# A tile of sparse attention moved among the query projections, and its output sums moved to GpSimd

## The chip, the cores and the metric

The kernel runs on one core of one Trainium2 chip. Times are device microseconds (us) of one execution of the whole program. TensorE (PE in the profile) multiplies matrices into PSUM, VectorE (DVE), ScalarE (ACT) and GpSimd (POOL) work on tiles, SyncE (SP) issues nearly all loads from HBM. Each engine works through its own queue in order, and waits where an instruction needs something that another engine or a load has not yet delivered.

## The reference

Two decoder layers over 512 tokens of width 1024. Layer 0 has latent attention, layer 1 sparse attention; each is followed by cross-attention into 256 memory tokens and a SwiGLU, with a residual and a layer norm after every sub-layer. All is float32. The change is in layer 1's sparse attention, 16 query heads in 4 groups that share keys and values:

```
def dsa_mixer(x, pos, rel_bias, w_in, w_o):
    h = x @ w_in          # -> q (16 heads x 64), k, v (4 x 64), q_idx (8 x 64), k_idx (64), w_idx (8)
    def one_block(...):   # 128 queries
        dots = einsum('bqhd,bkd->bqhk', qi_blk, k_idx) * 64 ** -0.5
        score = einsum('bqh,bqhk->bqk', wi_blk, relu(dots)); score = where(causal, score, -inf)
        _, sel = top_k(score, 128)                       # the keys of a query
        logits = einsum('bqngd,bqknd->bqngk', qg, k_sel) * 64 ** -0.5
        bias = rel_bias[t5_bucket(pos_blk - pos_sel)]
        p = softmax(where(sel_ok, logits + bias, -inf))
        return einsum('bqngk,bqknd->bqngd', p, v_sel)
    return blocks @ w_o
```

## The kernel before

A float32 product is made of reduced-precision ones: each operand is split into a high part (a rounding copy on ScalarE, `split`, line 98) and a low part (a subtraction on VectorE or GpSimd, line 100), and `mm3` (lines 121 to 123) adds three matmuls in PSUM. `chunk` loads 128x1024 weights into one of three raw buffers and splits them. The recording layer keeps each engine's queue roughly in the order of the source, but may put an instruction that it holds ready ahead of one that it holds late; within a queue nothing moves after that.

The sparse attention layer goes through these stages:

- Values, indexer keys and indexer queries are projected, and `masks[1]` to `masks[3]` collect the index scores of query tiles 1 to 3 (128 queries each; tile 0 needs only the causal mask).
- `topk` finds the 128 best keys of each query by 16 steps per tile. A step is a max of 8 and a replacement (lines 964, 965), both on VectorE; after the sixteenth, line 969 makes the mask. These 48 steps stand in `todo` and are handed out: 2 before each of the two key projections, `NTK` = 5 before each of the eight query projections, the last 4 in the item loop.
- Eight query projections (loop at line 1002), two heads each: 24 matmuls, then `stack_q_pool` with three copies on ScalarE and two subtractions on GpSimd. The weights' low parts are made on GpSimd too.
- 16 items, one for each query tile `qt` and key group `g`. `dsa_scores` (`run_s`) adds mask, and Q times both parts of K, for four heads, on PSUM banks of tag `b`; VectorE adds the bias and takes the maximum (line 410), ScalarE the exponential (416). Item i of tile 0 needs the heads 4i to 4i+3, so two query projections. `dsa_t` (`run_t`) spreads the reciprocal sums on GpSimd (421), transposes the probabilities on TensorE into banks of tag `a` and splits them. `dsa_pv` multiplies with the values: the high halves' sums are in partitions 0 to 63 of the bank `po`, the low halves' in 64 to 127.
- `out_proj` multiplies the outputs `OTd` with the output weights.

There are four PSUM banks of each tag, and 39 buffers of `t2` and 9 of `t8`; a tile waits until a buffer's last reader is done.

Of the kernel before, what the change touches and what calls it, by code (L numbers as in the profile page):

```python
# [12 lines left out]
FR = mybir.dt.float32r  # L13
I32 = mybir.dt.int32
AF = mybir.ActivationFunctionType
ALU = mybir.AluOpType
# [4 lines left out]
P = 128  # L21
# [3 lines left out]
NK = D // P  # L25
# [41 lines left out]
def tile_hybrid_mla_dsa_deepnorm_block(ctx: ExitStack, tc: tile.TileContext, A: dict, out: bass.AP):  # L67
    nc = tc.nc
# [13 lines left out]
    def t2(dt=F32, shape=(P, 512)):  # L82
        return tp.tile(list(shape), dt, tag="t2", name=nm("t2"), bufs=39)

    def t8(dt=FR, shape=(P, 4, 512)):
        return tp.tile(list(shape), dt, tag="t8", name=nm("t8"), bufs=9)
# [4 lines left out]
    def bank(tag, shape=(P, 512)):  # L91
        return pp.tile(list(shape), F32, tag=tag, name=nm("ps"))
# [14 lines left out]
    def chunk(src, shape, eng=None, after=(None, None)):  # L107
        n = int(np.prod(shape[1:]))
        raw = wp.tile([P, 1024], F32, tag="raw", name=nm("raw"), bufs=3)
        with behind(after[0]):  # L110
            nc.sync.dma_start(raw[:, :n], src)
        h = wp.tile([P, 1024], FR, tag="wh", name=nm("wh"))
        l = wp.tile([P, 1024], FR, tag="wl", name=nm("wl"))
        split(h[:, :n], l[:, :n], raw[:, :n], eng, after[1])
        if len(shape) == 2:
            return h[:, :n], l[:, :n]
        k = shape[1]
        return (h[:, :n].rearrange("p (k m) -> p k m", k=k), l[:, :n].rearrange("p (k m) -> p k m", k=k))
# [272 lines left out]
    def proj_tiles(ws, XT, halves):  # L391
        pss = [bank("a") for _ in ws]
        if halves:
            for cols in HALVES:
                for ps, w in zip(pss, ws):
                    proj(ps, w, XT, cols)
        else:
            for ps, w in zip(pss, ws):
                proj(ps, w, XT, (0, 512))
        return pss  # L400
# [34 lines left out]
    XT = [(t8(), t8()) for _ in range(2)]  # L435
# [41 lines left out]
    for c in range(4):  # L477
# [12 lines left out]
        for i in range(2):  # L490
            k = 2 * c + i
# [14 lines left out]
    steps = trig()  # L506
# [17 lines left out]
    OF = {}  # L524
# [141 lines left out]
    for h in range(16):  # L666
        PT = mla_t(h, Ss.pop(h))
# [45 lines left out]
    def cross(i, XT, m, kv0):  # L713
# [3 lines left out]
        def q_proj(hd):  # L717
            ws = [chunk(A["xa_q"][i, 2 * hd + dt], (P, NK, P)) for dt in range(2)]
            pq = proj_tiles(ws, XT, hd == 0)
            Q = []  # L720
            for dt in range(2):
                q = (t2(FR), t2(FR))
                split(q[0], q[1], pq[dt])
                Q.append(q)
            return Q

        def scores(hd, Q):
            Kt = kvs[hd][0]
# [164 lines left out]
    XT = norm.XT  # L893
# [8 lines left out]
    def stack_q_pool(ps, QA, QB):  # L902
        f = t2()
        nc.scalar.copy(f, ps)
        nc.scalar.copy(QA[0:64], ps[0:64])
        nc.scalar.copy(QB[64:128], ps[64:128])
        nc.gpsimd.tensor_tensor(QA[64:128], f[0:64], QA[0:64].bitcast(F32), op=ALU.subtract)
        nc.gpsimd.tensor_tensor(QB[0:64], f[64:128], QB[64:128].bitcast(F32), op=ALU.subtract)
# [50 lines left out]
    def topk(qt, its):  # L959
        n = P * (qt + 1)  # L960
        acc = masks[qt]
        for it in its:
            m8 = tp.tile([P, 8], F32, tag="m8", name=nm("m8"), bufs=4)
            nc.vector.max(out=m8, in_=acc[:, :n])  # L964
            nc.vector.match_replace(out=acc[:, :n], in_to_replace=m8, in_values=acc[:, :n], imm_value=-3e38)  # L965
        if its[-1] < TOPK // 8 - 1:
            return
        mk = MK[:, qt]
        nc.vector.tensor_scalar(mk[:, :n], acc[:, :n], -2e38, -BIG, op0=ALU.is_gt, op1=ALU.mult)
        masks[qt] = mk  # L970

    todo = [(qt, [i]) for qt in range(1, NT) for i in range(TOPK // 8)]
    NTK, NTI = 5, 1
# [16 lines left out]
    def dsa_bias(qt, g):  # L990
        n = P * (qt + 1)
        c0 = 127 + 384 - 128 * qt
        bt = t8(F32, (P, 4, 512)) if qt else t2(F32, (P, 4, P))
        read = nc.sync.dma_start(bt[:, :, 0:n],
                                 scr[bass.ds(r * (1 + qt), 1), 4 * g:4 * g + 4, :, c0:c0 + n].rearrange("a h p k -> p (a h) k"))
        reads.append(read)
        return bt

    Q = []
    q8 = t8()  # L1000
    first_bias, reads, spreads = [], [], []
    for j in range(8):
        if j >= 4:
            first_bias.append(dsa_bias(0, j - 4))
        for _ in range(min(NTK, len(todo))):
            topk(*todo.pop(0))
        (pq,) = proj_tiles([chunk(A["w_q"][j], (P, NK, P), nc.gpsimd)], XT, False)
        if j < 2:
            qa, qb = q8[:, 2 * j], q8[:, 2 * j + 1]
        else:  # L1010
            qa, qb = t2(FR), t2(FR)
        stack_q_pool(pq, qa, qb)
        Q += [qa, qb]

    OTd = []

    def new_outputs():
        o8 = t8()
        OTd.extend([(o8[:, 0], o8[:, 1]), (o8[:, 2], o8[:, 3])] + [(t2(FR), t2(FR)) for _ in range(NK - 2)])


    def dsa_scores(qt, g):
        n = P * (qt + 1)
# [28 lines left out]

    def dsa_pv(qt, g, rb, PT):
        ts_ = slice(P * qt, P * qt + P)
        po = bank("a")
        for kb in range(qt + 1):
            nc.tensor.matmul(po, VD[:, kb, g], PT[kb][0], start=(kb == 0), stop=False)
            nc.tensor.matmul(po, VD[:, kb, g], PT[kb][1], start=False, stop=(kb == qt))
        tmp = t2()
        nc.scalar.copy(tmp[0:64], po[64:128])  # L1060
        OF = t2(F32, (P, 2, P))
        ov = po[0:64].rearrange("p (i j q) -> p i j q", j=2, q=P)
        tv = tmp[0:64].rearrange("p (i j q) -> p i j q", j=2, q=P)
        for e in range(2):
            nc.vector.tensor_tensor(OF[64 * e:64 * e + 64], ov[:, :, e], tv[:, :, e], op=ALU.add)
        pr_ = bank("a", (P, 2, P))
        for i in range(2):
            nc.tensor.transpose(pr_[:, i], rb[:, 2 * i:2 * i + 2].rearrange("p a b -> p (a b)"), ident)
        nc.vector.tensor_tensor(OF, OF, pr_, op=ALU.mult)
        for i in range(2):  # L1070
            oh_, ol_ = OTd[2 * g + i]
            if qt < 3:
                nc.gpsimd.tensor_copy(oh_[:, ts_], OF[:, i])
                nc.gpsimd.tensor_tensor(ol_[:, ts_], OF[:, i], oh_[:, ts_].bitcast(F32), op=ALU.subtract)
            else:
                split(oh_[:, ts_], ol_[:, ts_], OF[:, i])


    items = [(qt, g) for qt in range(NT) for g in range(4)]
    LA = 12  # L1080
    Ss, PT = {}, {}

    def run_s(i):
        if i < 16:
            Ss[i] = dsa_scores(*items[i])

    def run_t(i):
        PT[i] = dsa_t(*items[i], Ss.pop(i))

    run_s(0)  # L1090
    run_s(1)
    run_t(0)
    new_outputs()
    for i in range(16):
        a = 1 if i < LA else 0
        if i != LA:
            run_s(i + 1 + a)
            run_t(i + a)
        dsa_pv(*items[i], *PT.pop(i))
        for _ in range(NTI):  # L1100
            if todo:
                topk(*todo.pop(0))
# [94 lines left out]
```

## Time and profile before

| what | value |
|---|---|
| median of 3 runs | 1549.07 us (1548.76 to 1550.13) |
| profiled execution, its time | 1550.88 us |
| its span (first to last instruction) | 1549.1 us |
| TensorE busy | 1510.6 us, 98% |
| VectorE, ScalarE, GpSimd busy | 64%, 42%, 21% |
| chain that ended last: TensorE, VectorE | 80%, 10% |

The profile comes from one execution, whose time lies 1.8 us above the median; terms read from it are differences within it. A matmul counts as busy until its modelled end, so that two which follow each other overlap: the pace of matmuls is read from their starts. The chain that ended last is followed back from the last instruction, at each step to what released it.

### The profile page before, as it was taken

How to read it: one execution, taken by the hardware profiler on the slowest of the kernel's cores; microseconds unless marked ns; L12 is line 12 of the kernel's file. 1: busy time of each engine (PE TensorE's matmuls, PEld its weight loads, DVE VectorE, ACT ScalarE, POOL GpSimd, SP SyncE). 2: the span in 40 equal slices, each digit the busy share in tenths (PEclk: the TensorE clock that was granted, in tenths of full speed). 3: DMA queues.
4: the chain of work that ended last, by engine and by line, in shares of the span. 5: the costliest groups of instructions: out<-in, count | busy, mean ns of one | idle time of the engine just before them, and what ended most of it. 6: DMA issues, size and time to landing. Idle time of an engine off the chain costs nothing.

```text
span 1549.1 us, 20803 instructions
## 1 busy us (share of the span) xinstructions
PE 1510.6 (98%) x7940; PEld 1290.5 (83%) x7940; DVE 996.6 (64%) x1709; ACT 650.1 (42%) x1150; POOL 321.8 (21%) x332
## 2 busy tenths in 40 slices
PE   9999999999999999999999899999999999999997
PEld 8788888988888888888888688898988888888886
DVE  6888868554746565654668979675548465656535
ACT  4677743343233333332246478334332333333320
POOL 2322101000132331400124553010002322324003
PEclk9999999999999999999999999999999999999999
DMA  6234424322323232223242337333323232322321
GB/s 221 71 99 110 147 82 139 120 87 91 130 88 116 75 121 86 98 90 109 83 150 69 96 109 245 109 109 110 109 90 128 78 113 94 106 94 88 96 94 55
DMA packets 51321, 166.79 MB, mean 108 GB/s; under 512 B 5300, under 2 KB 11748, under 8 KB 49172
## 3 DMA queue, kind: packets, MB, share of 16 engines
q1 hardware_dynamic: 50788, 164.41, 31.7%
q8 instruction: 62, 1.02, 0.3%
q10 hardware_dynamic: 432, 1.05, 0.2%
q14 instruction: 39, 0.32, 0.1%
HBM read 161.20 MB, written 9.47 MB: 110 GB/s over the span
## 4 chain that ended last, share of the span: by engine, by line
PE 80%; DVE 10%; ACT 3%; DMA 3%; issue 2%; POOL 1%; POOLq 0%; ACTq 0%; DVEq 0%; SPq 0%
PE ps L121 25%; PE ps L123 25%; PE ps L122 25%; DVE t L100 2%; DVE t L965 2%; DVE m L964 1%; ACT wh L98 1%; DVE wl L100 1%; ACT t L98 1%; PE ps L329 1%; PE ps L1047 1%; PE ps L1045 1%; POOL sm L272 1%; PE ps L1030 1%; ACT t L416 1%
## 5 line engine op out<-in xcount | busy, mean ns | idle before, releaser
L121 PE MATMUL ps<-t,wh 128*128 128x512 f32 (+1 forms) x1264 | 459.2, 363 | 3.4 <-DVE t L100 3.4
L122 PE MATMUL ps<-t,wh 128*128 128x512 f32 (+1 forms) x1264 | 458.1, 362 | 1.4 <-DVE t L100 1.4
L123 PE MATMUL ps<-t,wl 128*128 128x512 f32 (+1 forms) x1264 | 458.1, 362 | 0.0
L98 ACT CAST wh<-raw 128x1024 fp32r<-128x1024 f32 (+2 forms) x218 | 227.4, 1044 | 455.2 <-PE ps L122 168.2
L100 DVE TENSOR_TENSOR wl<-raw,wh 128x1024 fp32r<-128x1024 f32 (+2 forms) x197 | 253.2, 1287 | 226.7 <-ACT wh L98 224.9
L121 PE MATMUL ps<-wh,t 128*128 128x512 f32 (+2 forms) x838 | 305.0, 364 | 2.6 <-DVE t L100 1.5
L123 PE MATMUL ps<-wh,t 128*128 128x512 f32 (+2 forms) x838 | 303.1, 362 | 0.0
L122 PE MATMUL ps<-wl,t 128*128 128x512 f32 (+2 forms) x838 | 302.3, 361 | 0.0
L121 PEld LDWEIGHTS ps<-t,wh 128*128 128x128 f32 x1264 | 238.6, 189 | 41.8 <-DVE t L100 5.5
L122 PEld LDWEIGHTS ps<-t,wh 128*128 128x128 f32 x1264 | 238.6, 189 | 38.1 <-DVE t L100 1.9
L123 PEld LDWEIGHTS ps<-t,wl 128*128 128x128 f32 x1264 | 238.6, 189 | 37.2
L121 PEld LDWEIGHTS ps<-wh,t 128*128 128x128 f32 x838 | 159.0, 190 | 26.1 <-DVE t L100 1.7
L123 PEld LDWEIGHTS ps<-wh,t 128*128 128x128 f32 x838 | 158.9, 190 | 24.0 <-DVE t L100 0.5
L98 ACT CAST t<-ps 128x512 fp32r<-128x512 f32 (+2 forms) x249 | 122.9, 525 | 133.0 <-PE ps L329 87.8
L122 PEld LDWEIGHTS ps<-wl,t 128*128 128x128 f32 x838 | 159.1, 190 | 23.0
L270 POOL TENSOR_SCALAR sm<-sm 128x1 f32<-128x1 f32 x32 | 19.0, 594 | 674.7 <-DVE sm L304 634.5
L100 DVE TENSOR_TENSOR t<-ps,t 128x512 fp32r<-128x512 f32 (+2 forms) x249 | 144.1, 606 | 22.3 <-ACT t L98 20.7
L98 ACT CAST wh<-t 128x1024 fp32r<-128x1024 f32 x56 | 58.9, 1052 | 141.5 <-PE ps L122 123.5
L100 DVE TENSOR_TENSOR wl<-t,wh 128x1024 fp32r<-128x1024 f32 x56 | 71.2, 1272 | 64.8 <-ACT wh L98 63.1
L843 DVE TENSOR_TENSOR t<-ps,t 128x512 f32<-128x512 f32 x44 | 30.4, 692 | 120.4 <-PE ps L123 120.4
L100 DVE TENSOR_TENSOR t<-t,t 128x512 fp32r<-128x512 f32 (+2 forms) x113 | 83.9, 746 | 23.7 <-ACT t L98 21.5
L98 ACT CAST t<-t 128x512 fp32r<-128x512 f32 (+2 forms) x113 | 64.5, 574 | 57.7 <-POOL t L777 33.3
(177 smaller groups left out, 1690.5 us busy)
## 6 DMA issues: line engine op xcount, KB each, us to landing
raw<-in_ffn_in_dram SPq DMA_DIRECT2D x88, 512.0 KB, 3.2
t<-in_ffn_dg_dram SPq DMA_DIRECT2D x16, 1024.0 KB, 5.0
raw<-in_xa_k_dram SPq DMA_DIRECT2D x16, 512.0 KB, 3.2
raw<-in_xa_v_dram SPq DMA_DIRECT2D x16, 512.0 KB, 3.7
raw<-in_xa_q_dram SPq DMA_DIRECT2D x16, 512.0 KB, 3.7
raw<-in_xa_o_dram SPq DMA_DIRECT2D x16, 512.0 KB, 3.2
raw<-in_ffn_dl_dram SPq DMA_DIRECT2D x12, 512.0 KB, 3.2
scr<-vscr SPq DMA_DIRECT2D x16, 319.5 KB, 4.4
```

Source lines behind the costliest of these rows:

```text
L98: nc.scalar.copy(h, src)
L100: (eng or nc.vector).tensor_tensor(l, src, h.bitcast(F32), op=ALU.subtract)
L121: nc.tensor.matmul(ps, st[0], mv[0], start=start, stop=False, skip_group_check=more)
L122: nc.tensor.matmul(ps, st[0], mv[1], start=False, stop=False, skip_group_check=more)
L123: nc.tensor.matmul(ps, st[1], mv[0], start=False, stop=stop, skip_group_check=more)
L270: nc.gpsimd.tensor_scalar(a, var, scale, eps, op0=ALU.mult, op1=ALU.add)
L272: nc.gpsimd.tensor_tensor(b, a, mhalf, op=ALU.pow)
L329: nc.tensor.transpose(pt[:, k], x_of(tt)[:, 512 * n + P * k:512 * n + P * k + P], ident)
L416: nc.scalar.activation(Sx, src, AF.Exp, bias=nb, scale=scale, accum_out=self.sm[:, i:i + 1])
L843: nc.vector.tensor_tensor(sg, pu, sg, op=ALU.mult)
L964: nc.vector.max(out=m8, in_=acc[:, :n])
L965: nc.vector.match_replace(out=acc[:, :n], in_to_replace=m8, in_values=acc[:, :n], imm_value=-3e38)
```

## The change

The loop over the query projections is moved behind the definitions of the items' parts, and now also issues parts of the first tile's items: after projection 1 the scores of item 0, after 2 its transposes, after 3 the scores of item 1 and the output product of item 0, and so on by the table `steps`. The item loop starts at item 3. The tile-0 bias loads are issued before projections 0 to 3 instead of 4 to 7. In `dsa_pv`, for all 16 items, ScalarE copies both halves of `po` to SBUF (before: one half), and the two additions that make the sum run on GpSimd from SBUF (before: on VectorE from PSUM and SBUF). The output tiles of tile 0 are taken item by item; the pair in a `t8` tile is now that of heads 12 to 15.

```diff
--- before.py
+++ after.py
@@ -996,28 +996,9 @@
         reads.append(read)
         return bt
 
-    Q = []
+    Q, OTd = [], {}
     q8 = t8()
     first_bias, reads, spreads = [], [], []
-    for j in range(8):
-        if j >= 4:
-            first_bias.append(dsa_bias(0, j - 4))
-        for _ in range(min(NTK, len(todo))):
-            topk(*todo.pop(0))
-        (pq,) = proj_tiles([chunk(A["w_q"][j], (P, NK, P), nc.gpsimd)], XT, False)
-        if j < 2:
-            qa, qb = q8[:, 2 * j], q8[:, 2 * j + 1]
-        else:
-            qa, qb = t2(FR), t2(FR)
-        stack_q_pool(pq, qa, qb)
-        Q += [qa, qb]
-
-    OTd = []
-
-    def new_outputs():
-        o8 = t8()
-        OTd.extend([(o8[:, 0], o8[:, 1]), (o8[:, 2], o8[:, 3])] + [(t2(FR), t2(FR)) for _ in range(NK - 2)])
-
 
     def dsa_scores(qt, g):
         n = P * (qt + 1)
@@ -1052,17 +1033,25 @@
 
     def dsa_pv(qt, g, rb, PT):
         ts_ = slice(P * qt, P * qt + P)
+        if qt == 0:
+            if g < 3:
+                for k in (2 * g, 2 * g + 1):
+                    OTd[k] = t2(FR), t2(FR)
+            else:
+                o8 = t8()
+                OTd[6], OTd[7] = (o8[:, 0], o8[:, 1]), (o8[:, 2], o8[:, 3])
         po = bank("a")
         for kb in range(qt + 1):
             nc.tensor.matmul(po, VD[:, kb, g], PT[kb][0], start=(kb == 0), stop=False)
             nc.tensor.matmul(po, VD[:, kb, g], PT[kb][1], start=False, stop=(kb == qt))
-        tmp = t2()
-        nc.scalar.copy(tmp[0:64], po[64:128])
+        halves = []
+        for rows in (slice(64, 128), slice(0, 64)):
+            tmp = t2()
+            nc.scalar.copy(tmp[0:64], po[rows])
+            halves.append(tmp[0:64].rearrange("p (i j q) -> p i j q", j=2, q=P))
         OF = t2(F32, (P, 2, P))
-        ov = po[0:64].rearrange("p (i j q) -> p i j q", j=2, q=P)
-        tv = tmp[0:64].rearrange("p (i j q) -> p i j q", j=2, q=P)
         for e in range(2):
-            nc.vector.tensor_tensor(OF[64 * e:64 * e + 64], ov[:, :, e], tv[:, :, e], op=ALU.add)
+            nc.gpsimd.tensor_tensor(OF[64 * e:64 * e + 64], halves[1][:, :, e], halves[0][:, :, e], op=ALU.add)
         pr_ = bank("a", (P, 2, P))
         for i in range(2):
             nc.tensor.transpose(pr_[:, i], rb[:, 2 * i:2 * i + 2].rearrange("p a b -> p (a b)"), ident)
@@ -1087,11 +1076,34 @@
     def run_t(i):
         PT[i] = dsa_t(*items[i], Ss.pop(i))
 
-    run_s(0)
-    run_s(1)
-    run_t(0)
-    new_outputs()
-    for i in range(16):
+
+    steps = {1: "s0", 2: "t0", 3: "s1 p0", 4: "t1", 5: "s2 p1", 6: "t2", 7: "s3 p2"}
+
+    def run(word):
+        kind, i = word[0], int(word[1:])
+        if kind == "p":
+            dsa_pv(*items[i], *PT.pop(i))
+        else:
+            (run_s if kind == "s" else run_t)(i)
+
+    for j in range(8):
+        if j < 4:
+            first_bias.append(dsa_bias(0, j))
+        for _ in range(min(NTK, len(todo))):
+            topk(*todo.pop(0))
+        (pq,) = proj_tiles([chunk(A["w_q"][j], (P, NK, P), nc.gpsimd)], XT, False)
+        if j < 2:
+            qa, qb = q8[:, 2 * j], q8[:, 2 * j + 1]
+        else:
+            qa, qb = t2(FR), t2(FR)
+        stack_q_pool(pq, qa, qb)
+        Q += [qa, qb]
+        for word in steps.get(j, "").split():
+            run(word)
+
+    run_s(4)
+    run_t(3)
+    for i in range(3, 16):
         a = 1 if i < LA else 0
         if i != LA:
             run_s(i + 1 + a)
```

On TensorE, the last matmuls of the last query projection and what follows them, before:

```order
L122 MATMUL ps_11360<-t_1389_10065,wh_11356 128x512
L123 MATMUL ps_11360<-t_1388_10064,wl_11357 128x512
L1030 MATMUL ps_11395<-t_1536_10860,identr 128x256
L1031 MATMUL ps_11395<-t_1543_10899,t_1551_10954 128x256
L1032 MATMUL ps_11395<-t_1543_10899,t_1551_10954 128x256
```

and in the changed kernel the last matmuls of the second query projection (into `ps_11032`), with the third (`ps_11113`) behind:

```order
L122 MATMUL ps_11032<-t_1389_10065,wh_11028 128x512
L123 MATMUL ps_11032<-t_1388_10064,wl_11029 128x512
L1011 MATMUL ps_11065<-t_1536_10860,identr 128x256
L1012 MATMUL ps_11065<-t_1543_10899,t_1551_10954 128x256
L1013 MATMUL ps_11065<-t_1543_10899,t_1551_10954 128x256
L1011 MATMUL ps_11071<-t_1536_10860,identr 128x256
L1012 MATMUL ps_11071<-t_1543_10899,t_1551_10954 128x256
L1013 MATMUL ps_11071<-t_1543_10899,t_1551_10954 128x256
L1011 MATMUL ps_11077<-t_1536_10860,identr 128x256
L1011 MATMUL ps_11083<-t_1536_10860,identr 128x256
L121 MATMUL ps_11113<-t_1386_10062,wh_11109 128x512
```

Item 0's scores (mask, then both parts of K: lines 1011 to 1013, were 1030 to 1032) stand behind the second projection instead of the eighth; of its third and fourth head only the mask's matmul stands there, the rest is put among the third projection's matmuls.

On VectorE, where item 0's first two scores are read (ISA of line 410), before; `t_1462` holds tile 3's index scores:

```order
L964 MAX m_1639_11348<-t_1462_10553 128x8
L965 MATCH_REPLACE t_1462_10553<-m_1639_11348,t_1462_10553 128x512
L964 MAX m_1640_11351<-t_1462_10553 128x8
L410 ISA t_1596_11168,sm_11393<-ps_11395,t_1596_11168 128x128
L410 ISA sm_11393 128x1
L965 MATCH_REPLACE t_1462_10553<-m_1640_11351,t_1462_10553 128x512
L410 ISA t_1596_11168,sm_11393<-ps_11401,t_1596_11168 128x128
L410 ISA sm_11393 128x1
```

and in the changed kernel; `t_1460`, `t_1461` are those of tiles 1 and 2:

```order
L965 MATCH_REPLACE t_1461_10552<-m_1583_11098,t_1461_10552 128x384
L969 TENSOR_SCALAR t_1536_10860<-t_1460_10551 128x256
L964 MAX m_1584_11101<-t_1461_10552 128x8
L410 ISA t_1552_10955,sm_11063<-ps_11065,t_1552_10955 128x128
L410 ISA sm_11063 128x1
L410 ISA t_1552_10955,sm_11063<-ps_11071,t_1552_10955 128x128
L410 ISA sm_11063 128x1
L965 MATCH_REPLACE t_1461_10552<-m_1584_11101,t_1461_10552 128x384
```

It has moved from behind the twelfth max of tile 3 to behind the second max of tile 2.

On VectorE again, the first two items' output sums and products with the spread reciprocals, before:

```order
L969 TENSOR_SCALAR t_1536_10860<-t_1462_10553 128x512
L1065 TENSOR_TENSOR t_1691_11517<-ps_11512,t_1690_11515 64x256 x2
L1069 TENSOR_TENSOR t_1691_11517<-t_1691_11517,ps_11520 128x256
L1065 TENSOR_TENSOR t_1707_11576<-ps_11571,t_1706_11574 64x256 x2
L1069 TENSOR_TENSOR t_1707_11576<-t_1707_11576,ps_11579 128x256
```

and item 0's product in the changed kernel (line 1058, was 1069), between top-k steps, with GpSimd's queue around the sum that it waits for (line 1054):

```order
L964 MAX m_1645_11338<-t_1461_10552 128x8
L964 MAX m_1646_11342<-t_1462_10553 128x8
L1058 TENSOR_TENSOR t_1624_11253<-t_1624_11253,ps_11256 128x256
L420 RECIPROCAL sm_11319<-sm_11217 128x4
L965 MATCH_REPLACE t_1461_10552<-m_1645_11338,t_1461_10552 128x384
```

```order
L907 TENSOR_TENSOR t_1608_11208<-t_1610_11210,t_1608_11208 64x512
L908 TENSOR_TENSOR t_1609_11209<-t_1610_11210,t_1609_11209 64x512
L1054 TENSOR_TENSOR t_1624_11253<-t_1623_11251,t_1622_11249 64x256 x2
L1062 CAST t_1617_11242<-t_1624_11253 128x128
L1063 TENSOR_TENSOR t_1618_11243<-t_1624_11253,t_1617_11242 128x128
L1062 CAST t_1619_11244<-t_1624_11253 128x128
L1063 TENSOR_TENSOR t_1620_11245<-t_1624_11253,t_1619_11244 128x128
```

The sum has left VectorE's queue, and the product now stands between top-k steps there; on GpSimd the sum stands behind the subtractions of projection 3.

## Rows read from the trace of the kernel before

**Rows 1.** Windows: stretch, length, busy PE PEld DVE ACT POOL, clock, DMA share, GB/s.
```profile
856.00:881.00 25.00, 25.00 (x117) 20.90 (x116) 23.86 (x58) 10.90 (x18) 14.28 (x12) 1.00 0.28 86
...
881.00:895.00 14.00, 6.58 (x32) 6.22 (x31) 12.05 (x42) 5.25 (x18) 2.87 (x3) 0.63 0.22 73
...
895.00:906.00 11.00, 9.42 (x68) 8.07 (x67) 8.26 (x32) 7.65 (x25) 4.80 (x9) 1.00 0.14 49
...
918.00:978.00 60.00, 59.41 (x347) 49.47 (x346) 53.78 (x149) 49.40 (x120) 23.25 (x49) 1.00 0.61 211
```

**Rows 2.** Timeline of TensorE; columns: start, us, engine, line, op, shapes, idle before.
```profile
874.17 0.39 PE L121 MATMUL ps<-t,wh 128*128 128x512 f32 x1
...
879.61 0.28 PE L1030 MATMUL ps<-t,identr 128*128 128x256 f32 x1
...
880.92 0.28 PE L1032 MATMUL ps<-t,t 128*128 128x256 f32 x1
...
888.62 0.58 PE L1030 MATMUL ps<-t,identr 128*128 128x256 f32 x1 [7.42 <-DVE sm L410]
...
913.60 0.28 PE L1032 MATMUL ps<-t,t 128*128 128x256 f32 x1
...
918.17 0.42 PE L1030 MATMUL ps<-t,identr 128*128 128x384 f32 x1
...
919.98 2.06 PE L1045 MATMUL ps<-ident,t 128*128 128x128 f32 x16
```

**Rows 3.** Windows, two short ones in and after the hole.
```profile
886.00:888.00 2.00, 0.00 (x0) 0.00 (x0) 1.91 (x4) 0.00 (x0) 0.00 (x0) 0.50 0.00 0
...
895.00:896.00 1.00, 1.00 (x12) 1.00 (x11) 0.72 (x6) 0.86 (x3) 0.00 (x0) 1.00 0.00 0
```

**Rows 4.** Timeline of VectorE across the projections.
```profile
849.91 2.33 DVE L969 TENSOR_SCALAR t<-t 128x256 fp32r<-128x256 f32 x1
...
852.16 0.55 DVE L964 MAX8 m<-t 128x8 f32<-128x384 f32 x1
...
872.38 0.68 DVE L964 MAX8 m<-t 128x8 f32<-128x512 f32 x1
...
887.54 0.69 DVE L964 MAX8 m<-t 128x8 f32<-128x512 f32 x1
...
888.27 0.29 DVE L410 CUSTOM_DVE_ANT_0 t<-ps,t 128x128 f32<-128x128 f32 x1
...
900.67 0.43 DVE L969 TENSOR_SCALAR t<-t 128x512 fp32r<-128x512 f32 x1
```

**Rows 5.** Groups by form, VectorE, 820 to 985; columns: busy, mean ns | idle before.
```profile
L1065 DVE TENSOR_TENSOR t<-ps,t 64x256 f32<-64x256 f32 x32 | 13.3, 416 | 7.4 <-ACT t L1060 6.8 <-POOL wl L100 0.4
...
L1069 DVE TENSOR_TENSOR t<-t,ps 128x256 f32<-128x256 f32 x16 | 6.6, 416 | 0.2
...
L410 DVE CUSTOM_DVE_ANT_0 t<-ps,t 128x128 f32<-128x128 f32 x16 | 4.2, 286 | 2.3 <-PE ps L1032 2.2
```

**Rows 6.** Timeline of GpSimd across the projections.
```profile
846.96 1.29 POOL L907 TENSOR_TENSOR t<-t,t 64x512 fp32r<-64x512 f32 x1
...
848.32 1.29 POOL L908 TENSOR_TENSOR t<-t,t 64x512 fp32r<-64x512 f32 x1
...
849.69 2.40 POOL L100 TENSOR_TENSOR wl<-raw,wh 128x1024 fp32r<-128x1024 f32 x1
...
853.54 1.30 POOL L908 TENSOR_TENSOR t<-t,t 64x512 fp32r<-64x512 f32 x1
```

**Rows 7.** ScalarE's group by form, and line 776 (ns: least, median, most).
```profile
L1060 ACT COPY t<-ps 64x512 f32<-64x512 f32 x16 | 9.3, 583 | 6.5 <-PE ps L1058 6.3
...
L776 POOL TENSOR_TENSOR t<-t,t x16: 737/740/857, 445.0 to 1422.8; 128x256 f32<-128x256 f32 x16
```

**Rows 8.** Timeline, output product to scaled result of one item.
```profile
922.58 0.39 PE L1058 MATMUL ps<-t,t 128*128 128x512 f32 x1
...
925.22 0.42 DVE L1069 TENSOR_TENSOR t<-t,ps 128x256 f32<-128x256 f32 x1
```

## The prediction

> **What bounds the kernel now.** I read the page first: TensorE is busy 98% of the span, so only a stage in which it waits can give anything. The windows view of the sparse attention layer finds that stage [rows 1]: while the query projections run (856 to 881 us) TensorE is busy in all 25 us, in 881 to 895 it is busy 6.58 of 14 us at a granted clock of 0.63, and from 918 to 978 59.41 of 60. TensorE's timeline shows why [rows 2]. The eight projections take 5.44 us each (874.17 to 879.61, 24 matmuls at 0.227). Then come the scores of item 0, twelve 256-column matmuls in 1.43 us, and after them TensorE stands for 7.42 us until VectorE has read the first score. It resumes at a granted clock of 0.50, the lower (1.2 GHz) of its two levels, and is back at 2.4 GHz only by 895 [rows 3]: about 22 matmuls run at half pace there, some 3 us. In 895 to 906 another 1.6 us are idle [rows 1], and up to 1 us until 914. All losses of this front together: 7.4 + 3 + 2 to 3, about 13 us. That is the most that this change can win at its front.
>
> VectorE's timeline tells what TensorE waits for [rows 4]. VectorE works through the top-k of tiles 1 to 3 without a hole: the second max of tile 2 at 852.16, the second of tile 3 at 872.38, the twelfth at 887.54, and only then, at 888.27, the first score reduction. A top-k step of tile 3 costs (887.54 - 872.38) / 10 = 1.52 us. TensorE's hole is VectorE's backlog, which moving TensorE's work cannot shorten.
>
> **The change, part by part.** *Interleaving.* In the changed order the first reduction of item 0 stands on VectorE behind that second max of tile 2, so at about 852.7, 36 us earlier. But items 1, 2 and 3 stand between later top-k steps, so each of them comes when the top-k before it is done. The last top-k step ended by 900.67 in the kernel before. From 852.16 on that is 48.5 us, in which lie the 16 reductions of items 0 to 3 (0.21 us apart when back to back) and 2.3 us of waiting [rows 5]. In the changed kernel twelve of these reductions stand ahead of the end of top-k, and two products with the spread reciprocals (0.42 us each). So: 48.5 - 2.3 - 4 x 0.21 + 2 x 0.42 = 46.2. Two things are added. Each product now waits for ScalarE and GpSimd, 0.5 us by the order of the queues. And the mask instruction L969 took 2.33 us on 256 columns [rows 4], where its 512-column form took 0.43 at 900.67; a GpSimd subtraction ran from 849.69 to 852.09, exactly under it [rows 6]. With more GpSimd work beside the two later masks I add 0.5 (0 to 2 x 1.9). Sum 47.7: item 3's first score is read at 899.9.
>
> The page "SBUF — State Buffer", section "Who interferes with whom", of the Trainium skill says that such a VectorE instruction and a GpSimd one exclude each other for a whole instruction; the 2.33 us agree, and by the rule alone both later masks could wait for a whole GpSimd instruction, which would be the upper end just named.
>
> *TensorE up to there.* Its work ahead of item 3's scores is done: projections to 879.6 if nothing waits, plus scores of items 0 to 3 (4 x 1.43), transposes of items 0 to 2 (8 matmuls each, at 0.12 by the sixteen in 2.06 us at 919.98 [rows 2], so 0.96), three low-half matmuls (0.23) and three output products (0.45 + 0.25): 11.4 us, so 891.0. It does wait: item 0's scores need the first two projections' Q, and GpSimd delivers these at 849.6 and 854.8 [rows 6], since three weight subtractions stand ahead; TensorE could use them at 847 and 849.4. With the Q of the later pairs (0.6 to 0.9 us late) that is 5 to 7 us of waiting, in pieces under 2 us, and TensorE arrives at 897 to 898: still ahead of VectorE's 899.9. So these waits cost nothing, up to 2 us more of them too; beyond that each one counts. In the kernel before no other stall of this stage lowered the clock, so I take full clock there.
>
> *After it.* Item 4's first score needs the bank of item 3's first, 900.1. From there to the end of item 7's scores TensorE has 12.6 us of work: scores of items 4 to 7 5.7, transposes of items 3 to 5 (one, two and two key blocks) 4.8, products and low half of items 3 and 4 2.1. I add 1.0 us of waits (item 3's and item 4's exponentials, which stand behind the copies of the outputs on ScalarE): 913.7. The kernel before ends item 7's scores at 913.72 [rows 2], but has not yet done item 5's transposes and item 4's product, which the changed kernel has; that is done when it starts L1030 at 918.17, less three 384-column matmuls of item 8 that stand before it there and not in the changed kernel (0.17 each, 0.5): 917.65. Gain 4.0 us.
>
> *Output sums, all 16 items.* Off VectorE: 32 additions of 0.416, 13.3 us [rows 5]. Onto ScalarE: one more copy of 64x512 each, 16 x 0.58 = 9.3 us [rows 7]. Onto GpSimd: 32 additions of 64x256, not in the trace; the nearest row is the 128x256 sum, 0.74 us [rows 7]; the 64x512 ones, 1.29 each (846.96 to 848.25) [rows 6], bound it above and zero below; I take 0.74, 23.7 us in all, on an engine that is busy 23 of 60 us [rows 1]. In 918 to 978 TensorE has hardly a hole, so relief of VectorE (53.8 of 60 busy) is worth at most 0.6 us of idling there and perhaps 1 us of shorter delays. ScalarE goes from 49.4 to about 56 of 60 us. The chain from an output product to its scaled result took 922.58 to 925.64 [rows 8]; it grows by 0.58 + 1.48 - 0.83 = 1.2 us per item. TensorE covers it as long as the transposed reciprocals' bank isn't wanted back: four banks of tag a serve two to four transposes, a product and this one, and at tile 2 and 3 an item lasts 5 to 7 us on TensorE against a chain of about 4. I charge 0.3 us net for all of this.
>
> The GPSIMD Engine Reference of the Trainium skill, section 4.1, advises against this edit: elementwise work on two inputs is about twice as slow there as on VectorE. The rows agree (0.74 on 128x256 beside 0.416). Charged in full to the path it would be 32 x 0.32 = 10 us and the kernel slower; what decides is cover, not the rate.
>
> *Nothing at the rest.* The first tile's bias loads move ahead of weight loads on SP's queue, where the DMA engines are used at a share of 0.28 [rows 1], so nothing is short; top-k steps in the item loop fall on items 3 to 6 instead of 0 to 3, and tile 3's mask is wanted only at item 12.
>
> Sum: -4.0 + 0.3 = -3.7 us. The profiled execution took 1550.88 us (span 1549.1); 1547.2 is expected of the like, and the median, 1.8 below it, goes from 1549.07 to **1545.4 us**.
>
> **Rivals.** *A: the whole front is recovered.* The backlog is not the limit but the order was; the hole, the half clock and the later stalls go: 10 to 13 us, 1537 to 1539. For it: TensorE's own work ends at 891.0. Against: VectorE has no hole to give, 23.86 of 25 us busy and then 12.05 of 14 [rows 1].
> *B: the longer chain takes over.* VectorE's product waits in its queue for GpSimd, the score reductions behind it wait too, and TensorE waits for them; with ScalarE near full this is repeated at each of the 12 items after the front. At the full 1.2 us each it is 14 us against the 4 gained, 1559; at half, 1552. It decides from 0.35 us per item. For it: VectorE and TensorE are both over 85% busy, so a wait has little room. Against: VectorE is relieved by 0.84 per item in the same loop, and TensorE's only stalls after 918 are short.
> *C: no change.* The early waits of TensorE grow past their 2 us of cover (its clock falls in them, say, costing the 3 us seen once), or the mask waits 2 us twice: 4 us, and the gain is gone: 1549.
>
> **How the numbers follow.** Forecast (gain 2 to 7) 0.50, A 0.10, C 0.22, B 0.18. The forecast's own range is 1542 to 1547; reaching into A and half of B gives 1539.5 to 1552. Under 0.2% (3.1 us) this kernel's time can't be told from no change. Of the forecast 0.42 lies beyond it, with A 0.10 and a bit of C: faster 0.54. Within: the rest of the forecast and most of C, 0.27. Slower: B and a little of C, 0.19.
>
> **What would show it.** Right: the first score reduction near 853; the last top-k step still near 900; TensorE's stalls at 847 to 856 under 2 us each and one of about 2 us before item 4's scores, no stretch at clock 0.5; GpSimd's sums at 0.7 us each; TensorE in the last 60 us of the items as full as before. Wrong: the last top-k step far from 900 (VectorE's sum), a lowered clock between 847 and 857 (C), or VectorE waiting for GpSimd for more than 0.4 us per item with TensorE idle beside it (B).

## The result, and the profile after

The changed kernel takes 1557.18 us (median of 6 runs, 1556.50 to 1560.34), the kernel before 1548.98 (6 runs, 1548.69 to 1552.16): ratio 1.0052, 95% interval 1.0041 to 1.0062. It is 8.2 us slower, and outside the range of the prediction. The profiled execution took 1556.50 us, with a span of 1554.7 against 1549.1 before. The two spans differ by 5.6 us only, since before's profiled execution lay 1.9 us above its median and this one 0.7 below; the first of the marks below allows for that.

The windows of the layer come first, in the stretches of [rows 1] and one ahead of them (846 to 856, where TensorE was busy 10.00 of 10 us before); the columns are the length, then the busy time of PE, PEld, DVE, ACT and POOL, the granted clock, the DMA share and GB/s.

```profile
846.00:856.00 10.00, 7.63 (x29) 5.48 (x29) 9.73 (x31) 5.69 (x13) 7.31 (x5) 0.83 0.41 134
856.00:881.00 25.00, 23.18 (x114) 18.51 (x113) 23.04 (x64) 13.13 (x26) 15.68 (x16) 1.00 0.10 32
881.00:895.00 14.00, 12.31 (x57) 9.75 (x55) 11.82 (x33) 7.45 (x18) 7.14 (x11) 0.88 0.00 1
895.00:906.00 11.00, 9.42 (x55) 7.91 (x55) 7.13 (x27) 5.58 (x16) 4.41 (x5) 1.00 0.44 143
918.00:978.00 60.00, 53.64 (x309) 43.74 (x308) 41.14 (x117) 51.92 (x127) 35.03 (x64) 1.00 0.60 207
```

The hole at 881 to 895 is gone: 12.31 of 14 us busy instead of 6.58. But TensorE now loses time before it, and above all after it: in 918 to 978 it is busy 53.64 of 60 us, where it was 59.41. VectorE is relieved there as forecast (53.78 to 41.14), and the time is worse.

Three marks on TensorE split the 8 us (columns as in [rows 2]). The first is the last matmul of the second query projection, the last one before TensorE's order differs, in the kernel before and then in the changed one:

```profile
846.74 0.39 PE L123 MATMUL ps<-t,wl 128*128 128x512 f32 x1
```

```profile
845.61 0.39 PE L123 MATMUL ps<-t,wl 128*128 128x512 f32 x1
```

So the changed kernel's profiled execution is 1.13 us ahead before any change to TensorE's order (it was 1.17 ahead at the layer norm in front of this layer). The second mark is where item 8's first score starts, that is, where items 0 to 7 have their scores:

```profile
916.98 0.36 PE L1011 MATMUL ps<-t,identr 128*128 128x384 f32 x1
```

In the kernel before the like point was 917.65, as the prediction worked out. Of the lead of 1.13 us 0.67 is left: the front lost 0.5 us. The third mark is the first transposition of the last token tile's layer norm, behind the output projection, here in the kernel before and then in the changed one:

```profile
1029.26 0.41 PE L329 MATMUL ps<-ident,t 128*128 128x128 f32 x2 [1.04 <-DVE t L325]
```

```profile
1036.41 0.41 PE L329 MATMUL ps<-ident,t 128*128 128x128 f32 x2 [1.32 <-DVE t L325]
```

There it is 7.15 us late. So some 7.8 us were lost between, in items 4 to 15 and the output projection. With the front's 0.5 that makes 8.3, close to the 8.2 of the medians. The list of waits for 918 to 986 us names what (columns: who waited, for whom, us in total, times, longest):

```profile
DVE t L1058 <- POOL t L1054: 17.6, 11, 3.8
...
PE ps L1028 <- DVE t L1058: 3.6, 5, 1.1
PE ps L1045 <- DVE t L1058: 2.7, 3, 1.5
```

VectorE's product (L1058) stood waiting for GpSimd's sum 11 times, 1.6 us each, and TensorE waited for that product 6.3 us. One such item, on ScalarE, GpSimd, VectorE and TensorE in turn:

```profile
929.13 1.19 ACT L1050 COPY t<-ps 64x512 f32<-64x512 f32 x2
...
929.19 2.40 POOL L100 TENSOR_TENSOR wl<-raw,wh 128x1024 fp32r<-128x1024 f32 x1
931.55 1.52 POOL L1054 TENSOR_TENSOR t<-t,t 64x256 f32<-64x256 f32 x2
...
933.10 0.42 DVE L1058 TENSOR_TENSOR t<-t,ps 128x256 f32<-128x256 f32 x1 [1.08 <-POOL t L1054]
933.44 0.55 DVE L410 CUSTOM_DVE_ANT_0 t<-ps,t 128x384 f32<-128x384 f32 x1
...
934.87 0.69 DVE L100 TENSOR_TENSOR t<-ps,t 128x512 fp32r<-128x512 f32 x1
...
933.67 0.47 PE L1045 MATMUL ps<-t,t 128*128 128x512 f32 x1 [1.52 <-DVE t L1058]
```

The copies are done at 930.32. The sum starts only at 931.55, since GpSimd's queue had begun a weight subtraction of 2.40 us. VectorE waits, and three score reductions (the first is shown) and a split stand behind the product. TensorE stands 1.52 us.

In the front, TensorE waits for Q from GpSimd (lines 907, 908) in pieces of about 1 us, and twice runs at half clock afterwards; the timeline, and the clock in two short windows:

```profile
847.16 0.39 PE L1012 MATMUL ps<-t,t 128*128 128x256 f32 x1 [1.05 <-POOL t L907]
...
848.51 0.39 PE L1012 MATMUL ps<-t,t 128*128 128x256 f32 x1 [0.72 <-POOL t L908]
...
902.53 0.39 PE L1012 MATMUL ps<-t,t 128*128 128x256 f32 x1 [0.81 <-POOL t L907]
...
903.88 0.39 PE L1012 MATMUL ps<-t,t 128*128 128x256 f32 x1 [0.61 <-POOL t L908]
```

```profile
850.00:852.00 2.00, 2.00 (x6) 1.32 (x4) 1.97 (x7) 0.12 (x1) 1.92 (x2) 0.50 0.05 16
888.00:890.00 2.00, 2.00 (x6) 1.59 (x5) 1.97 (x6) 0.15 (x2) 1.21 (x3) 0.51 0.00 0
```

VectorE's timeline, to be held against [rows 4], has the first reduction and the last top-k step where the prediction put them (near 853, near 900), but VectorE then waits for TensorE, and not the other way round:

```profile
851.55 0.29 DVE L410 CUSTOM_DVE_ANT_0 t<-ps,t 128x128 f32<-128x128 f32 x1
...
898.50 0.68 DVE L965 MATCH_REPLACE8 t<-m,t 128x512 f32<-128x512 f32 x1
900.35 0.29 DVE L410 CUSTOM_DVE_ANT_0 t<-ps,t 128x128 f32<-128x128 f32 x1 [1.18 <-PE ps L1013]
...
903.07 0.29 DVE L410 CUSTOM_DVE_ANT_0 t<-ps,t 128x128 f32<-128x128 f32 x1 [1.72 <-PE ps L1013]
```

### The profile page after: what moved, and what is told of

The parts are those of the page before. It is cut to its first block, busy times and chain, and to the rows that moved or that the text cites. A ratio compares the mean times of both kernels' runs of the same rounds, so it can differ in the third digit from the quotient of the medians.

```text
span 1554.7 us, 20837 instructions
## 1 busy us (share of the span) xinstructions
PE 1512.1 (97%) x7940; PEld 1287.0 (83%) x7940; DVE 983.7 (63%) x1677; ACT 657.7 (42%) x1166; POOL 345.7 (22%) x364
## 3 DMA queue, kind: packets, MB, share of 16 engines
q10 hardware_dynamic: 432, 1.05, 0.2%
## 4 chain that ended last, share of the span: by engine, by line
PE 80%; DVE 7%; ACT 5%; POOL 4%; issue 3%; DMA 1%; POOLq 0%; SPq 0%; ACTq 0%; DVEq 0%
PE ps L121 25%; PE ps L123 25%; PE ps L122 25%; DVE t L100 2%; ACT t L416 1%; ACT t L98 1%; ACT wh L98 1%; POOL t L1054 1%; DVE wl L100 1%; POOL wl L100 1%; PE ps L329 1%; POOL sm L272 1%; DVE t L325 1%; POOL sm L270 1%; PE ps L624 1%
```

## The experiments

Twelve kernels, in three groups of four; each group was timed beside the kernel before on the same chip (medians 1549.40, 1549.18 and 1549.35 us).

| kernel | median us | ratio to before, 95% interval |
|---|---|---|
| interleave alone | 1549.06 | 1.0000 (0.9990 to 1.0009) |
| sums alone | 1562.85 | 1.0086 (1.0073 to 1.0100) |
| both copies, additions on VectorE | 1553.39 | 1.0026 (1.0016 to 1.0036) |
| product on GpSimd too | 1557.49 | 1.0057 (1.0043 to 1.0071) |
| early copy, product on VectorE | 1556.53 | 1.0047 (1.0033 to 1.0060) |
| product and last tile's splits on GpSimd | 1550.91 | 1.0008 (0.9998 to 1.0017) |
| shifted interleave, old sums | 1546.32 | 0.9979 (0.9970 to 0.9988) |
| shifted, fewer top-k steps per projection | 1545.76 | 0.9977 (0.9968 to 0.9986) |
| kernel before, 8 top-k steps left out | 1543.70 | 0.9962 (0.9949 to 0.9976) |
| shifted, 8 top-k steps left out | 1541.61 | 0.9946 (0.9932 to 0.9959) |
| shifted, tile 0's sums on GpSimd | 1546.23 | 0.9981 (0.9972 to 0.9990) |
| shifted, all sums on GpSimd | 1546.39 | 0.9981 (0.9972 to 0.9990) |

### The two halves apart

The interleave alone keeps the order of the changed kernel and takes back the sums:

```diff
-        halves = []
-        for rows in (slice(64, 128), slice(0, 64)):
...
-            nc.gpsimd.tensor_tensor(OF[64 * e:64 * e + 64], halves[1][:, :, e], halves[0][:, :, e], op=ALU.add)
+        tmp = t2()
+        nc.scalar.copy(tmp[0:64], po[64:128])
...
+            nc.vector.tensor_tensor(OF[64 * e:64 * e + 64], ov[:, :, e], tv[:, :, e], op=ALU.add)
```

> The interleaved order of the changed kernel with the output sums of the kernel before (one ScalarE copy, two additions on VectorE from PSUM). Theory 1, the longer chain: the 7 to 8 us lost against the kernel before are all in items 4 to 15, where VectorE's product waits for GpSimd and the PSUM bank of the transposed reciprocals with it; the interleave by itself gains next to nothing, because TensorE's waits for Q and its half clock eat the hole that they replace. So 1548 to 1550, and no wait of TensorE for the product above 0.3 us. Theory 2, the order itself costs (items in other places of the queues): 1554 to 1557. Theory 3, my forecast's front was right and hidden: about 1545.

The sums alone are the same edit the other way, in the kernel before.

> The order of the kernel before, with only the output sums changed (two ScalarE copies, additions on GpSimd). Theory 1 (the chain): 1555 to 1558, with TensorE waiting for the products of VectorE by 6 us or more in sum between items 1 and 15, and the hole before the first tile's reductions unchanged at 7 us. Theory 2 (the order): 1548 to 1550.

The interleave alone gains nothing: 1549.06. The sums alone cost 13.4 us, more than theory 1 expected (10.8 us between the first and the last mark of its profiled execution, which lies 2.4 us below its median). The windows of 918 to 978 us, first with the interleave alone, then with the sums alone:

```profile
918.00:978.00 60.00, 59.07 (x345) 49.31 (x344) 53.50 (x149) 50.40 (x125) 20.69 (x45) 1.00 0.60 213
```

```profile
918.00:978.00 60.00, 53.66 (x313) 43.82 (x312) 39.84 (x118) 51.19 (x126) 37.77 (x69) 1.00 0.62 211
```

With the old sums TensorE is full again; with the new ones it has the same holes in either order. That is theory 1's division of the loss. In the old order the sums cost more, since tile 0's four items pay too: there TensorE is busy 17.96 of the 23 us from 895 to 918, where it was 20.92 of 23 in the kernel before (9.42 + 11.50), and the hole ahead is unchanged (7.41 us). These 3 us and the 7.8 of items 4 to 15 make up the 10.8. What theory 1 missed is that the interleave spares the first four items this.

### Which part of the sums

First GpSimd's additions go back to VectorE, now from SBUF, with both ScalarE copies kept:

```diff
-            nc.gpsimd.tensor_tensor(OF[64 * e:64 * e + 64], halves[1][:, :, e], halves[0][:, :, e], op=ALU.add)
+            nc.vector.tensor_tensor(OF[64 * e:64 * e + 64], halves[1][:, :, e], halves[0][:, :, e], op=ALU.add)
```

> The changed kernel with both ScalarE copies, but the two additions on VectorE, from SBUF. It tells the second copy from GpSimd's additions. Theory 1a, GpSimd's 1.5 us and VectorE's wait for it are what holds the bank: the chain is 0.6 us longer than before instead of 1.2, and the two engines' handing over is gone: 1549 to 1552. Theory 1b, ScalarE's second copy is what makes the chain late: 1555 to 1557, as the changed kernel.

1553.39 lies between the two answers: over the interleave alone, the second copy with SBUF operands costs 4.3 us here, and GpSimd's additions the other 3.8. VectorE waits 8.8 us for the copies (4.5 before). And two of the additions took longer than their 0.42 us, 1.53 and 0.77, both while GpSimd made a weight subtraction. VectorE, GpSimd and TensorE at the first:

```profile
928.66 1.96 DVE L1054 TENSOR_TENSOR t<-t,t 64x256 f32<-64x256 f32 x2
...
930.75 0.53 DVE L410 CUSTOM_DVE_ANT_0 t<-ps,t 128x384 f32<-128x384 f32 x1
...
927.51 2.40 POOL L100 TENSOR_TENSOR wl<-raw,wh 128x1024 fp32r<-128x1024 f32 x1
...
931.34 0.44 PE L1011 MATMUL ps<-t,identr 128*128 128x384 f32 x1 [1.23 <-DVE sm L410]
```

The first of the pair took 1.53 us, the longest of this line's 32, and TensorE waits 1.23 us for the reduction behind them. In the kernel before one operand is in PSUM, and none of the 32 additions took over 0.42.

The next two ask what holds TensorE: the PSUM bank that the product keeps, or VectorE's queue that stands still. In both VectorE copies the transposed reciprocals out of the bank at once; the product then runs on GpSimd, or on VectorE.

```diff
-        nc.vector.tensor_tensor(OF, OF, pr_, op=ALU.mult)
+        pc = t2(F32, (P, 2, P))
+        nc.vector.tensor_copy(pc, pr_)
+        nc.gpsimd.tensor_tensor(OF, OF, pc, op=ALU.mult)    # in the other: nc.vector
```

> The changed kernel, but VectorE copies the transposed reciprocals out of PSUM at once, and the product runs on GpSimd too, from SBUF. The bank no longer waits for the sum, and VectorE no longer waits for GpSimd; the chain itself grows by a GpSimd product of about 0.75 us. Theory 1 (what costs is the bank held and VectorE's queue stopped, not the length of the chain): 1547 to 1550. Rival: the length of the chain or GpSimd's load decides: 1556 to 1560.

> The changed kernel, but VectorE copies the transposed reciprocals out of PSUM at once, and makes the product later from SBUF: the bank is free early, VectorE still waits for GpSimd's sum, with the score reductions and splits of the next items behind it. Theory 1a, the bank held is what costs: 1549 to 1552, as after the run with the product on GpSimd up to 960 us. Theory 1b, VectorE's stopped queue is what costs: 1555 to 1559 with VectorE's waits for GpSimd still 15 us or more in sum, and TensorE waiting for its reductions (line 410) or splits (line 100) instead of its product.

With the product on VectorE nothing is won (1556.53, in theory 1b's range). VectorE's waits from 918 to 986 are 13.0 us, less than the 15 expected and the 17.6 of the changed kernel. The bank is free, and TensorE waits for the splits behind the product instead:

```profile
DVE t L1060 <- POOL t L1054: 13.0, 9, 3.3
...
PE ps L1045 <- DVE t L100: 2.9, 3, 1.6
PE ps L1057 <- DVE t L100: 0.8, 2, 0.4
PE ps L1011 <- DVE sm L410: 0.6, 2, 0.4
```

So an early free bank does not help while the queue is stopped. But the time of the other kernel, 1557.49, in its rival's range, seems to speak against the stopped queue. Its windows show where:

```profile
918.00:948.00 30.00, 29.07 (x178) 24.81 (x176) 21.80 (x65) 28.88 (x71) 26.41 (x45) 1.00 0.70 243
948.00:978.00 30.00, 25.26 (x130) 20.05 (x131) 19.52 (x53) 21.17 (x51) 15.65 (x30) 0.94 0.46 167
```

Until 948 TensorE is full. From tile 3 on, the outputs are split by ScalarE (line 98), and now it is ScalarE that stands, with three splits of probabilities behind (ScalarE, then TensorE):

```profile
965.73 0.50 ACT L98 CAST t<-t 128x128 fp32r<-128x128 f32 x2 [3.39 <-POOL t L1060]
966.14 1.55 ACT L98 CAST t<-ps 128x512 fp32r<-128x512 f32 x3
...
966.77 0.80 PE L1045 MATMUL ps<-t,t 128*128 128x512 f32 x1 [2.84 <-ACT t L98]
```

If that reading is right, GpSimd should make these splits too:

```diff
-            if qt < 3:
+            if True:
                 nc.gpsimd.tensor_copy(oh_[:, ts_], OF[:, i])
```

> As the run with the product on GpSimd, and in addition the last query tile's outputs are split on GpSimd instead of ScalarE and VectorE: now no engine but GpSimd waits for GpSimd's sums. In the run before, TensorE waited 8 us between 946 and 985 us, for ScalarE's and VectorE's splits of probabilities that stood behind a split of the output waiting for GpSimd. If a stopped queue is what costs, these waits go: 1548.5 to 1551, TensorE 29 of 30 us busy in 948 to 978. If GpSimd's load (26 of 30 us in 918 to 948) or the longer chain decides: 1555 to 1559, TensorE still waiting, or the output projection late by the chain.

1550.91, and TensorE has 28.61 of the 30 us:

```profile
948.00:978.00 30.00, 28.61 (x165) 23.18 (x164) 21.32 (x54) 25.50 (x58) 21.47 (x44) 1.00 0.54 196
```

The longest chain of all, with GpSimd busiest (46.88 of 60 us in 918 to 978, against 35.03 in the changed kernel), costs about 1.9 us over VectorE's sums. So most of the 8 us is neither the chain's length nor GpSimd's load, but that an engine which feeds TensorE stands at the head of its queue waiting for GpSimd. The halves of 4.3 and 3.8 us above are not prices that add up: both ScalarE copies and the SBUF operands are still here. What the last 1.9 us are was not tested.

### What ate the front's gain

Each step comes one projection later, and item (1, 0), which needs the first two projections only, changes places with item (0, 3); the sums are those of before.

```diff
-    steps = {1: "s0", 2: "t0", 3: "s1 p0", 4: "t1", 5: "s2 p1", 6: "t2", 7: "s3 p2"}
+    steps = {2: "s0", 3: "t0", 4: "s1 p0", 5: "t1", 6: "s2 p1", 7: "t2 s3 p2"}
...
+    items[3], items[4] = items[4], items[3]
```

> The interleave alone (sums as in the kernel before), each step one projection later, and the first item of tile 1 (which needs the first two projections only) ahead of the last one of tile 0. TensorE's waits for Q (7.9 us at lines 907, 908) and the half clock behind them should go, if these are what eats the interleave's gain: TensorE is at the end of the projections by 892, and waits next for VectorE's top-k (near 898): 1543 to 1546. If TensorE's waits are only another face of VectorE's backlog: 1548 to 1550.

1546.32: 2.9 us under the kernel before, 0.3 above the range expected. The shift and the exchange of the two items were made together, so what each is worth is not shown. TensorE's waits from 836 to 918, with the interleave unshifted, then shifted:

```profile
PE ps L1012 <- POOL t L907: 4.8, 5, 1.5
PE ps L1012 <- POOL t L908: 3.2, 5, 0.7
```

```profile
PE ps L121 <- DVE t L1053: 1.7, 1, 1.7
PE ps L1011 <- DVE sm L410: 1.5, 1, 1.5
PE ps L1046 <- DVE t L100: 0.8, 1, 0.8
PE ps L1046 <- ACT t L105: 0.7, 1, 0.7
PE ps L1012 <- POOL t L908: 0.7, 1, 0.7
```

The 8.0 us for Q become 0.9, and 4 us of waiting for VectorE come in their place. A stretch at half clock remains, behind waits of 1.46 and 0.73 us for VectorE and ScalarE (a granted clock of 0.59 from 898 to 902). Two more kernels ask whether that is the backlog of top-k steps. One hands out fewer steps per projection:

```diff
-    NTK, NTI = 5, 1
+    NTK, NTI = 4, 2
```

> As the shifted interleave, and four top-k steps ahead of each query projection instead of five; the eight steps of tile 3 left over (12 us of VectorE) come in the item loop, two per item. If VectorE's backlog is the next limit, TensorE's wait at the end of the projections goes too: 1539 to 1543. If VectorE has no room in the item loop (26 to 27 of 30 us busy there): 1545 to 1550, with TensorE waiting for score reductions in 900 to 930.

1545.76 lies in the second range, and is no change from 1546.32 that the intervals tell apart. It doesn't decide: the recording layer put the steps forward, and VectorE is as busy as without the edit (13.54 of 14 us in 881 to 895, and 13.50). The other way is to leave work out, in the kernel before and in the shifted one:

```diff
-    todo = [(qt, [i]) for qt in range(1, NT) for i in range(TOPK // 8)]
+    todo = [(qt, [i]) for qt in range(1, NT) for i in range(8 * (qt == 3), TOPK // 8)]
```

> The kernel before with eight of tile 3's sixteen top-k steps left out (tile 3 then selects 64 keys instead of 128), about 12 us of VectorE. My prediction said that TensorE's hole of 7.4 us at 881 to 889 is VectorE's backlog of these steps. If so, the hole shrinks to below 1.5 us, the stretch at half clock behind it goes, and the time falls to 1538 to 1542. If the hole belongs to the chain of the first scores itself (reduction, exponential, banks): hole still 4 us or more, 1545 to 1549.

> The shifted interleave with the same eight top-k steps left out (tile 3 selects 64 keys). In the shifted interleave VectorE was busy 37.6 of 39 us between 856 and 895, TensorE's waits for Q are 1 us, and its waits for VectorE between 870 and 912 about 5 us with a stretch at half clock at 898 to 901. Moving the steps in the source had changed little, since they were put forward in VectorE's queue. If VectorE's backlog is now the limit of the front: 1538 to 1542. If it isn't: 1545 to 1547.

The shifted kernel gave 1541.61, as expected of a backlog that limits the front. The kernel before fell to 1543.70 only, between its two ranges, and its hole (7.42 us, [rows 2]) to 3.02:

```profile
883.65 0.58 PE L1030 MATMUL ps<-t,identr 128*128 128x256 f32 x1 [3.02 <-DVE sm L410]
```

With a cut of 12 us on VectorE ahead of the first reduction the hole should have vanished. VectorE's timeline of this run shows that more than half of the cut lay behind it:

```profile
881.71 0.68 DVE L965 MATCH_REPLACE8 t<-m,t 128x512 f32<-128x512 f32 x1
882.42 0.85 DVE L969 TENSOR_SCALAR t<-t 128x512 fp32r<-128x512 f32 x1
883.30 0.29 DVE L410 CUSTOM_DVE_ANT_0 t<-ps,t 128x128 f32<-128x128 f32 x1
```

In the kernel before the first reduction stands behind the twelfth max of tile 3 ([rows 4]: 887.54 and 888.27). Here it stands behind all eight steps that are left, and behind the mask of line 969, without idle time between. So only three and a half steps of 1.52 us, less 0.85 for the mask, have gone from ahead of it: 4.5 us, and the hole shrank by 4.4. The score that it reads was written by 879.6, so the 3.02 us that remain are backlog too.

### Two versions with both ideas

For tile 0 alone, sums and product on GpSimd, and ScalarE empties both banks:

```diff
+        if qt == 0:
+            pc = t2(F32, (P, 2, P))
+            nc.scalar.copy(pc, pr_)
+            nc.gpsimd.tensor_tensor(OF, OF, pc, op=ALU.mult)
+        else:
             nc.vector.tensor_tensor(OF, OF, pr_, op=ALU.mult)
```

> The shifted interleave, and for the four items of tile 0 alone the sums and the product on GpSimd, ScalarE copying both halves and the transposed reciprocals out of PSUM; the other twelve items as in the kernel before. VectorE is spared 4 x 1.25 us in its backlog, no engine but GpSimd waits for GpSimd, and the bank that TensorE waited for at 874 us (1.7 us, for additions of VectorE behind top-k steps) is freed by ScalarE. If a stopped queue is the price of a hand-over and VectorE the limit of the front: 1542 to 1545. If GpSimd is the limit (it makes Q and the weights' low parts too): 1547 to 1550.

> The shifted interleave with all sixteen items' sums, products and splits on GpSimd (VectorE only copies the transposed reciprocals). In the unshifted order this took 1.9 us more than VectorE's sums. If that is the price in the items after the front, and the front gains the 2 to 3 us of the shift: 1546 to 1549. If VectorE's relief in the front adds to it: 1543 to 1546.

1546.23 and 1546.39: both faster than the kernel before, neither told apart from the shifted interleave with the old sums. The first lies between its two ranges, the second in the range without a gain from VectorE's relief. In the front they trade waits (with tile 0's sums alone on GpSimd: 1.7 us of line 104 waiting for ScalarE, 1.1 for GpSimd's spread) for those on VectorE. The simplest version that beats both kernels is the shifted interleave with the sums left on VectorE.

## Why the prediction was wrong

- **The step that failed: output sums, "I charge 0.3 us net for all of this".** The runs show 8.1 us (changed kernel against the interleave alone, 1557.18 and 1549.06). Every duration in the step was right: the addition 0.73 us for 0.74, the copy 0.58, VectorE relieved. I asked only whether the bank of the transposed reciprocals would be wanted back, and the bank alone isn't the price: freeing it early, with VectorE's queue still stopped, changed 0.7 us, within the intervals. I had named the right mechanism in rival B (the product waits in VectorE's queue, the reductions behind it wait too) and given it 0.18. Its price fell at half of the full 1.2 us: 7.8 us over 12 items, 0.65 each.
- **Why it was underrated.** "Against: VectorE is relieved by 0.84 per item" set busy time against waiting time. VectorE had 19 of 60 us idle after the change and still made TensorE wait, because the idle time lay ahead of the product. And the chain was priced as a sum of durations; GpSimd's weight subtractions of 2.40 us were in [rows 6], and I did not add that one can stand ahead of a sum.
- **The reason given on ScalarE's copy was incomplete.** It was counted as 9.3 us of an engine with room. With the additions on VectorE, which then waits for the copies, it and the move of the operands to SBUF cost 4.3 us; with the whole tail on GpSimd, where both stay, all together cost 1.9.
- **The second step that failed: front, -4.0.** Measured +0.5 between the marks in the profile, and no change with the interleave alone (1549.06, against 1549.40 before). VectorE's sum was right: its last top-k step ends at 899.2, or 900.3 with the 1.1 us by which this execution was ahead; forecast 899.9. TensorE's was not: I had it there at 897 to 898 after 5 to 7 us of waiting, at full clock. The waits for Q were of that size (6.8 us ahead of 904), but it ran at half clock twice, so that the projections ended at 899.8 (900.9 with the lead), and item 3's third and fourth score waited for Q until 902.53 and 903.88. No other engine's work covers that last pair; I had not counted it. This is rival C's mechanism.
- **"TensorE's hole is VectorE's backlog"** was right: with steps left out the hole shrank by what left VectorE's queue ahead of the first reduction (4.5 us, 4.4 measured), and VectorE had no idle time in the rest.
- **Right:** the orders of instructions and every unit price; masks of tiles 2 and 3 beside more GpSimd work took 0.35 and 0.42 us, nothing of the 1.9 us each that I had allowed for; bias loads and moved top-k steps show no wait in the front.
- The GPSIMD Engine Reference of the Trainium skill, section 4.1, advised against elementwise work on two inputs on GpSimd for its rate. The advice was right here, the ground wasn't what decided: with the product and splits there as well, the same additions (0.73 us each) cost 1.9 us instead of 8.

## What to carry to other kernels

Work handed to another engine is priced by who waits for it at the head of which queue: put the whole tail on the engine that gets it, or nothing. Here even the whole tail gained nothing over sums left on VectorE (1546.39 and 1546.32). Before a consumer is moved up among its producers, count how long each producer's last step (here GpSimd's share of Q, with weight subtractions queued ahead) takes to arrive; here one step later, with two items exchanged, was worth some 3 us. Compare two traces from a mark ahead of the change: here a lead of 1.1 us made a loss in the front look like a gain. When an engine becomes less busy and nothing gets faster, look at what stands behind its longest wait.

## What the runs showed of the hardware

- Two VectorE additions of 64x256 that read only SBUF took 1.96 us, where other pairs took 0.85, while a GpSimd subtraction ran; with one operand in PSUM they took 0.41 to 0.42 each in all 32 cases of the kernel before, two of them (920.82 and 921.25) inside a GpSimd subtraction of 2.38 us that began at 919.51. The page "SBUF — State Buffer" of the Trainium skill, section "Who interferes with whom", says that a VectorE instruction with two inputs in SBUF contends with a GpSimd one that reads SBUF; these traces agree, and show that a copy out of PSUM for the sake of another engine can bring it on.
- TensorE's granted clock fell to 0.50, its lower level (1.2 GHz), behind waits of 1.05 and 0.72 us at 846 to 848.5, and to 0.51 behind two like ones at 884 to 886.5. In the kernel before, of this layer's waits only the hole of 7.42 us had done that. Short waits among dense work are not free, but not each of them costs the clock: behind those of 0.81 and 0.61 us ahead of 904, and behind the 1.52 us ahead of 933.67, it stayed at 1.00.
